# Three entries of a slot calendar moved: parts of y sooner, the last pair's values later, weight splits ahead of squares

## The chip, the cores and the metric

The kernel runs on one core of one Trainium2 chip. The metric is the device time of one execution in microseconds (us): before the change the median of 3 runs is 815.99 us (815.72 to 816.66).

## The reference

One decoder layer on x of 512 tokens and 2048 channels, in float32. What matters of it:

```python
h = rms_norm(x, norm_g)
a_val, a_glu, a_gate, q, k, v, b_gate = jnp.split(h @ w_in, SPLIT_POINTS, axis=-1)
u = a_val * jax.nn.sigmoid(a_glu)
u = causal_depthwise_conv(u, conv_w, conv_b)                   # 31 taps
u = jax.nn.silu(layer_norm(u, conv_norm_g, conv_norm_b))
y_a = (u @ conv_pw_w + conv_pw_b) * jax.nn.silu(a_gate)
o = dilated_attention_mixture(rms_norm(q), rms_norm(k), v)     # 16 heads of 64
y_b = o * jax.nn.silu(b_gate)
return x + jnp.concatenate([y_a, y_b], axis=-1) @ w_out
```

`w_in` is 2048 x 7168, `conv_pw_w` 1024 x 1024, `w_out` 2048 x 2048.

## The kernel before

**Products.** A float32 product is done as three float16 matmuls: both operands are scaled by a power of two and split into a high half (on ACT, an ACTIVATE copy to float16) and a low half (on DVE, what the copy left over), and `tri` (L414 to L416) adds high x high, high x low and low x high in PSUM. `split_hi` and `split_lo` (L298, L306) make `wh` and `wl` of a pass's weights. A pass is four blocks of 128 rows of a weight matrix by 512 columns. Its scale needs the sum of its squares (`measure`, L192, ACTIVATE into `junk`), and so do the scales of y.

**Order.** The program is written out by hand: nothing reorders it, and each engine takes its instructions in the order in which they are issued. The clock of that order is the slot, eight of them to a pass: a slot issues what is due in a calendar, what its pass has listed for it and some steps of the convolution branch, then six matmuls of 128x512 on PE. `after(n, fn)` puts `fn` into the calendar n slots on (at least one). In the loop over the plain passes (L1351) each slot takes two lists: `due`, from the calendar, and `extra`, the splits of the next pass's weights (high half at slot 0, low half at slot 2) and loads of the residual `res`. L1419 says which of the two comes first.

**Where the change sits.** The passes around it, in their order, are 52 to 55 (`bg` 1: the second half of the attention gate), 56 to 59 (`pw`: the pointwise projection of the convolution branch, 56 and 57 its first 512 columns, 58 and 59 its second), 60 and 61 (`wb` 2 and 3: rows 8 to 11 of y times `w_out`, plain, three matmuls to a block), and then four groups `wa` in Strassen's manner, seven products of halves instead of eight, whose weight blocks `ws`, `wsc` and `wsd` are sums made by DMAs that add (issued on GpSimd) and by DVE. The slots of `pw` start at 448, those of `wb` at 480, those of `wa` at 496.

**Names.** `cv` is the convolution's result in eight row blocks: the layer norm multiplies it by `lnrow` (DVE), applies SiLU (ACT, L609), and splits it into `u` (ACT L316, then DVE), which `pw` reads. Rows 8 to 11 of y are `y_b` of the first eight heads, in four tiles of `gate` ("b0"). `b0_parts` (L691) makes their halves: `plain` (L678) for `wb`, a high half on ACT (L688) and a low half on DVE for each of four tiles; and for `wa` the differences `ysum` of halves of these tiles (`y_sums`, L643, four pairs of subtractions on DVE), split by `block` (L663; ACT L675, then DVE) into four more parts. It asks for nothing but these tiles and the scale `yb0`, which is found by slot 360.

**Attention.** Heads go in pairs, a pair every 32 slots; pair 7, the last, begins at slot 450. Its scores (L741) come in two batches, at slots 450 and 453; DVE adds the table to them and takes them out of PSUM (`sx<-ps_s`). Then follow the exponentials (ACT L754), the two halves of the probabilities (`hl`: ACT L765, then DVE), and a transposing DMA for each head on SyncE (`turn`, L774) into `pt`. `values` (L782) are 60 thin matmuls of `pt` with v into `ps_o`; `put` multiplies the outcome by the gate on DVE (`gate<-ps_o`) and hands it to `put_y` (L623), which has ACT square it. When all twelve tiles of `y_a` and of the later `y_b` are squared, the scale `yabs` is found and `y_parts` (L701) makes the halves for `wa`. `end_pair` issues `values` and `put`; it is due when the next pair begins, and for pair 7 after `PERIOD - 2` slots, at 480.

**Buffers.** PSUM has four banks for `ps_l` (L102) and four for `ps_s` and `ps_o` (L103), which are taken in turn: a batch of scores waits until DVE has read what stood in its banks. Tiles of y, u, gate and cv rotate through one pool of 35 slots; halves of weights through 4 buffers, so that `wh` of the next pass waits until PE is done with the pass before this one.

Of the kernel before, what the change touches and what calls it, by code (L numbers as in the profile page):

```python
# [35 lines left out]
PERIOD = {0: 32, 1: 32}  # L36
# [50 lines left out]
def layer(ctx: ExitStack, tc: tile.TileContext, xt, w1, w2, w3, g_in, conv_w, conv_b,  # L87
# [31 lines left out]
    calendar = {}  # L119
    clock = [-1]  # L120

    def after(n, fn):

        calendar.setdefault(clock[0] + max(n, 1), []).append(fn)
# [126 lines left out]
    of_group = {}  # L251
# [46 lines left out]
    def split_hi(i):  # L298
        if i < n_plain:
            parts[i] = [part_pool.tile([P, KU, S], F16, name=n, tag="part") for n in ("wh", "wl")]  # L300
            A.activation(parts[i][0], raw[i], AF.Copy, scale=wscale[units[i][3:]][0])  # L301
# [4 lines left out]
    def split_lo(i):  # L306
        if i < n_plain:
            wh, wl = parts[i]
            V.scalar_tensor_tensor(wl, raw.pop(i), wscale[units[i][3:]][0], wh, op0=OP.mult, op1=OP.subtract)
            load(i + RING)  # L310
            after(11 if of_next(i) in SEVEN else 9, lambda: measure(i + RING))
# [110 lines left out]
    def evac_scale(group):  # L422

        if group not in escale:
            other = {"pw": "u", "wa": "yab", "wb": "yb0"}.get(group[0])
            e = escale[group] = small.tile([P, 1], F32, name="esc")
            G.tensor_tensor(e, wscale[group][1], scales[other][1] if other else xinv, op=OP.mult)
        return escale[group]
# [377 lines left out]
    def end_pair(pair):  # L806

        for fn in to_come.pop(pair, ()):
            fn()

    def attention(hf):
        start = max(clock[0] + 28, max(at_pair.values(), default=0) + PERIOD[0])
        start += (PHASE - start) % 8
        for p4 in range(4):
            at_pair[4 * hf + p4] = start + p4 * PERIOD[hf]

            def begin(pair=4 * hf + p4):
                end_pair(pair - 1)
                plan, values, put = two_heads(pair)
                to_come[pair] = values, put  # L820
                for n, fn in plan:
                    if n == 0:
                        fn()
                    else:
                        after(n, fn)
                after(PERIOD[hf] - 2 * (pair == 7), lambda: end_pair(pair))
            after(at_pair[4 * hf + p4] - clock[0], begin)


# [31 lines left out]
    def fetch_res(j):  # L861

        res[j] = wide_tile("res", [P, 2, S], F32)
        nc.sync.dma_start(res[j], rows_of(xt, j))
# [4 lines left out]
    def run_conv():  # L869

        pace = PACE_2 if 0 < min(at_pair.values(), default=0) <= clock[0] else PACE
        V.load = min(max(V.load - pace, -pace), 4 * pace)
        wait[0] -= 1
        while (V.load < 0 or wait[1]) and wait[0] <= 0:
            n = next(convolution, 1)
            if n:
                wait[0] = n
# [442 lines left out]
    def startup(n):  # L1320

        s, second = divmod(n, 2)
        todo = []
        if not second:
            if s + 3 < KU * n_exact:
                todo += [lambda: exact_hi(s + 3), lambda: exact_lo(s + 3)]
            if s + 2 < KC:
                todo.append(lambda: split_x(s + 2))
        if n == 0:
            for k in range(1, KC):  # L1330
                after(4 + (k - 1) * 26 // 14, lambda k=k: square_x(k))
            for n in range(KC):
                after(NORM_FROM + n * (70 - NORM_FROM) // KC, lambda k=n // 2 + 4 * (n // 8) + 4 * (n % 2): norm_x(k))
            for j in range(8):
                after(SUM_FROM + SUM_STEP * j // 2, lambda j=j: sum_x(j))
            g = token_rsqrt(xacc, D, RMS_EPS, rstd, rrow)
            for m in (32, 33, 36):
                after(m, lambda: next(g, None))
            for m, fn in ((21, x_consts), (40, score_consts), (37, u_consts)):
                after(m, fn)  # L1340
            after(8 * n_exact - 4, lambda: split_hi(n_exact))
            after(8 * n_exact - 3, lambda: split_lo(n_exact))
        return todo
# [3 lines left out]
    def due_now():  # L1347
        return [fn for n in sorted(n for n in calendar if n <= clock[0]) for fn in calendar.pop(n)]

    calendar.setdefault(8 * of_group["pw", 0][0] + 6, []).append(b0_parts)  # L1350
    for i in range(n_plain):  # L1351
        kind, g = group = units[i][3:]
        if group in SEVEN:
            if i == of_group[group][0]:
                plan = ahead.pop(i) + later
                later = []
                n_next = i + 4
                if units[n_next][3:] in SEVEN:
                    ahead[n_next] = input_products(n_next)
                    plan += [(n + 28, fn) for n, fn in ahead[n_next] if n < 0]  # L1360
                else:
                    plan = [(24, lambda: split_hi(n_next)), (25, lambda: split_lo(n_next))] + plan
                for n in range(28):
                    clock[0] = 8 * i + n + n // 7
                    for fn in due_now():
                        fn()
                    first = [fn for k, fn in plan if k == n]
                    for fn in first[:]:
                        if fn.__name__ != "matmuls":
                            fn()  # L1370
                    run_conv()
                    for fn in first:
                        if fn.__name__ == "matmuls":
                            fn()
                later = [(n - 28, fn) for n, fn in plan if n >= 28]
                if units[n_next][3:] not in SEVEN:
                    for n, fn in later:
                        after(8 * n_next + n - clock[0], fn)
                    later = []
                if kind == "k":  # L1380
                    attention(g)
            continue
        exact = i < n_exact
        if exact:
            order = [(None, None)] * 8
        else:
            order = [(m, hf) for m in range(4) for hf in range(2)]
            extra = [[] for _ in range(8)]
            if i == n_plain - 1:
                for n, fn in seven_parts(0):  # L1390
                    if n < 0:
                        extra[n].append(fn)
            if i + 1 < len(units) and units[i + 1][3:] in SEVEN:
                ahead[i + 1] = input_products(i + 1)
                for n, fn in ahead[i + 1]:
                    if n < 0:
                        extra[n].append(fn)
            else:
                extra[0].append(lambda: split_hi(i + 1))
                extra[2].append(lambda: split_lo(i + 1))  # L1400
            if i + 1 < len(units) and units[i + 1][3] == "wb":
                for m in range(2):
                    extra[4 * m].append(lambda m=m: fetch_res(2 * units[i + 1][4] + m))
            if kind == "pw" and i == n_plain - 3:
                for n in (2, 3):
                    extra[n].append(lambda n=n: evac_scale(("wb", n)))
            if (kind, g) == ("wb", 3):
                for m in range(2):
                    extra[4 * m].append(lambda m=m: fetch_res(m))
        if kind == "pw":  # L1410
            need = KU * units[i][2] + KU - 1
            while need not in u16:
                next(convolution)
        for n, (m, hf) in enumerate(order):
            clock[0] = 8 * i + n
            if exact:
                extra = {n: startup(clock[0])}
            due = due_now()
            for fn in extra[n] + due if exact else due + extra[n]:  # L1419
                fn()  # L1420
            run_conv()
            done = exact_matmuls(clock[0]) if exact else slot_matmuls(i, m, hf)
            if done:
                done()
        if kind == "k" and i == of_group[group][-1]:
            attention(g)
# [62 lines left out]
```

## Time and profile before

| | before |
|---|---|
| median of 3 runs | 815.99 us (815.72 to 816.66) |
| the profiled execution | 816.64 us |
| its span, first to last instruction | 814.5 us |
| mean granted TensorE clock | 0.998 |
| PE busy | 806.0 us |
| DVE busy | 706.8 us |
| ACT busy | 561.5 us |
| GpSimd busy | 136.8 us |

Times in the profile are us from the span's start; a line such as L414 is that of the code above. A row of the timeline is: start, duration, engine, line, operation, out<-in, shape and count; in brackets the idle time of the engine before it and who ended it. Rows of ACT and DVE overlap a little, and a matmul of 128x512 is shown with 0.38 us though they start 0.22 apart. A row of the windows is: stretch, its length, then the busy time of PE, its weight loads, DVE, ACT and GpSimd, the granted clock, the DMAs' share and GB/s. SPq rows are transfers that SyncE issues.

### The profile page before, as it was taken

The page shows a single profiled execution, that of the slowest core. Times are in us where ns is not written, and L with a number is a line of the kernel's source. Part 1 is how long each engine was busy: PE and PEld are TensorE (multiplying, and loading weights), DVE is VectorE, ACT ScalarE, POOL GpSimd, SP SyncE. Part 2 cuts the span into 40 slices and gives each one's busy share as a digit, 9 for nine tenths or more (in the row PEclk, how much of TensorE's full clock was granted, in tenths as well). Part 3 has the DMA queues.
Part 4 walks back from the last instruction along what each step waited for, and adds up shares of the span by engine and source line. Part 5 has one row for each costly group of instructions (what it writes and reads, how often), then busy time and mean ns, then how long its engine had stood idle before and what let it go on. Part 6 is the DMA issues. An engine that isn't in the chain of part 4 may idle for free.

```text
span 814.5 us, 13602 instructions
## 1 busy us (share of the span) xinstructions
PE 806.0 (99%) x5341; PEld 509.4 (63%) x5341; DVE 706.8 (87%) x1188; ACT 561.5 (69%) x788; POOL 136.8 (17%) x147
## 2 busy tenths in 40 slices
PE   9999999999999999999999999999999989999998
PEld 6887745888646854444444444444444446888887
DVE  6768999878989889999999989996579889978885
ACT  6667687577756688586747657497799849864641
POOL 0001021322224300004012010000200003423420
PEclk9999999999999999999999999999999999999999
DMA  9852346993874863526494624425361467898752
GB/s 338 330 233 98 109 104 137 144 248 55 315 149 100 148 261 113 123 93 164 142 181 130 151 97 137 135 89 133 104 168 63 126 213 195 162 259 201 130 102 68
DMA packets 100000, 127.19 MB, mean 156 GB/s; under 512 B 62560, under 2 KB 85344, under 8 KB 90720
## 3 DMA queue, kind: packets, MB, share of 16 engines
q1 hardware_dynamic: 80544, 107.37, 42.2%
q0 software_dynamic: 19104, 18.88, 16.2%
q8 instruction: 41, 0.67, 0.3%
q14 instruction: 23, 0.19, 0.1%
q10 hardware_dynamic: 288, 0.07, 0.0%
HBM read 88.56 MB, written 4.19 MB: 114 GB/s over the span
## 4 chain that ended last, share of the span: by engine, by line
PE 90%; DVE 3%; ACT 3%; DMA 2%; issue 1%; POOL 0%; SPq 0%; ACTq 0%; DVEq 0%
PE ps_l L414 24%; PE ps_l L415 23%; PE ps_l L416 23%; PE ps_l L895 10%; PE ps_s L416 2%; PE ps_s L415 2%; PE ps_s L414 2%; PE ps_o L782 2%; PE ps_s L741 2%; ACT junk L192 1%; DVE ws L82 1%; DMA wf<-w_dram 1%; DMA pt<-hl 1%; ACT sx L754 1%; DVE wl L82 1%
## 5 line engine op out<-in xcount | busy, mean ns | idle before, releaser
L82 DVE SCALAR_TENSOR_TENSOR cv<-u,cw,cv 128x511 f32<-128x511 f32 (+14 forms) x240 | 161.9, 727 | 0.4 <-ACT cv L552 0.4
L192 ACT ACTIVATE junk<-wf 128x2048 uint8<-128x2048 f32 x68 | 129.2, 1899 | 10.4 <-DMA wf<-w_dram 10.0
L414 PE MATMUL ps_l<-x,wh 128*128 128x512 f16 x320 | 121.3, 379 | 0.4 <-DVE glu L82 0.4
L416 PE MATMUL ps_l<-x,wl 128*128 128x512 f16 x320 | 121.3, 379 | 0.0
L415 PE MATMUL ps_l<-x,wh 128*128 128x512 f16 x320 | 121.3, 379 | 0.0
L301 ACT ACTIVATE wh<-wf,ws 128x2048 f16<-128x2048 f32 x42 | 83.8, 1994 | 53.3 <-PE ps_l L415 51.5
L82 DVE SCALAR_TENSOR_TENSOR wl<-wf,ws,wh 128x2048 f16<-128x2048 f32 x43 | 100.9, 2346 | 11.5 <-ACT wh L301 11.5
L414 PE MATMUL ps_l<-wh,x 128*128 128x512 f16 x256 | 97.1, 379 | 0.0
L416 PE MATMUL ps_l<-wh,x 128*128 128x512 f16 x256 | 97.0, 379 | 0.0
L415 PE MATMUL ps_l<-wl,x 128*128 128x512 f16 x256 | 97.0, 379 | 0.0
L82 DVE SCALAR_TENSOR_TENSOR ws<-wf,ws 128x1024 f16<-128x1024 f32 x70 | 89.1, 1278 | 7.3 <-ACT ws L1173 4.5
L414 PEld LDWEIGHTS <-wh 128*128 128x128 f16 x448 | 43.9, 98 | 51.5 <-issue 4.0
L416 PEld LDWEIGHTS <-wl 128*128 128x128 f16 x448 | 43.8, 98 | 51.1 <-DVE wl L82 1.9
L415 PEld LDWEIGHTS <-wh 128*128 128x128 f16 x448 | 43.8, 98 | 47.1 <-issue 0.8
L895 PE MATMUL ps_l<-xr,wr 128*128 128x512 f32 x288 | 69.4, 396 | 0.5 <-ACT xr L339 0.5
L895 PEld LDWEIGHTS ps_l<-xr,wr 128*128 128x128 f32 x288 | 53.9, 188 | 14.2 <-ACT xr L339 1.8
L206 POOL TENSOR_SCALAR ws<-ws 128x1 f32<-128x1 f32 x20 | 9.8, 488 | 309.1 <-DVE ws L82 308.7
L414 PEld LDWEIGHTS <-x 128*128 128x128 f16 x352 | 34.4, 98 | 32.5 <-issue 1.9
L416 PEld LDWEIGHTS <-x 128*128 128x128 f16 x352 | 34.4, 98 | 31.3
L415 PEld LDWEIGHTS <-x 128*128 128x128 f16 x352 | 34.4, 98 | 30.1
L1173 ACT ACTIVATE ws<-wf,ws 128x1024 f16<-128x1024 f32 x42 | 47.1, 1138 | 5.7 <-PE ps_l L416 4.8
L170 POOL TENSOR_TENSOR ss<-ss,half 128x8 f32<-128x8 f32 x16 | 31.5, 1970 | 116.8 <-DVE ss L82 116.6
(265 smaller groups left out, 1872.9 us busy)
## 6 DMA issues: line engine op xcount, KB each, us to landing
wf<-w_dram SPq DMA_DIRECT2D x72, 1024.0 KB, 5.2
wf<-wf POOLq DMA_DIRECT2D x30, 512.0 KB, 6.2
x<-xt_dram SPq DMA_DIRECT2D x16, 256.0 KB, 6.9
res<-xt_dram SPq DMA_DIRECT2D x8, 512.0 KB, 6.7
out_dram<-res SPq DMA_DIRECT2D x15, 256.0 KB, 3.7
wf<-w_dram SPq DMA_DIRECT2D x7, 512.0 KB, 7.2
wf<-wf POOLq DMA_DIRECT2D x12, 256.0 KB, 5.8
wf<-w_dram SPq DMA_DIRECT2D x2, 256.0 KB, 3.5
```

The costliest lines, as they stand in the source:

```text
L82: return getattr(self.engine, name)(out, src, *args, **kw)
L170: G.tensor_tensor(ap, ap, half.to_broadcast(list(ap.shape)), op=OP.pow)
L192: A.activation(junk[:, :n], src, AF.Square, scale=scale, accum_out=acc)
L206: G.tensor_scalar(scale, scale, 1e-30, 2.0 ** (-2 * top), op0=OP.max, op1=OP.mult)
L301: A.activation(parts[i][0], raw[i], AF.Copy, scale=wscale[units[i][3:]][0])
L414: T.matmul(ps, ah, bh, start=first, stop=False, skip_group_check=more)
L415: T.matmul(ps, ah, bl, start=False, stop=False, skip_group_check=more)
L416: T.matmul(ps, al, bh, start=False, stop=last, skip_group_check=more)
L741: T.matmul(ps[i, a], qk["q", hf][p4 // 2][rows, p4 % 2, q, i * P:w], qk["k", hf][p4 // 2][rows, p4 % 2, k, :w], start=n == 0, stop=n == 2)
L782: T.matmul(po[rows, i * P:(i + 1) * P], vs[hf][j // 2][:, j % 2, 2 * p4 + a, vp * DH:(vp + 1) * DH], got["t", a][:, pp * (ALL // P) + FROM ...
L895: T.matmul(banks[group, m], wt[:, a, m * P:(m + 1) * P], xk[b], start=k == 0 and a == b == 0, stop=k == KC - 1 and a == 1)
L1173: A.activation(t[:, 0], block(name, pair), AF.Copy, scale=wscale[group][0])
```

## The change

Three edits:

```diff
-                after(PERIOD[hf] - 2 * (pair == 7), lambda: end_pair(pair))
+                after(PERIOD[hf] - (pair == 7), lambda: end_pair(pair))
...
-    calendar.setdefault(8 * of_group["pw", 0][0] + 6, []).append(b0_parts)
+    calendar.setdefault(8 * of_group["pw", 0][0] - 10, []).append(b0_parts)
...
-            for fn in extra[n] + due if exact else due + extra[n]:
+            for fn in extra[n] + due if exact or kind == "wb" else due + extra[n]:
```

`b0_parts` starts at slot 438 instead of 454, in the last pass of the gate, where the layer norm's last steps run. Pair 7's values are issued at slot 481 instead of 480, so behind the first slot of `wb`. In the two `wb` passes the splits of the next weights stand ahead of what the calendar has for the slot. Nothing is added or left out; GpSimd's and SyncE's instructions stand as before.

On DVE, at the layer norm's end and pair 7's first scores. The number in a name tells one buffer from another (u_6090 before and u_6114 after are the same part of u); `gate<-ps_o` takes out the values of pair 6, `ISA sx` the scores. Before:

```order
L82 SCALAR_TENSOR_TENSOR u_6050<-cv,us,u_6050 128x512
L82 SCALAR_TENSOR_TENSOR gate<-opair,osc,gate 128x512
L82 TENSOR_TENSOR cv<-cv,lnrow 128x512
L82 SCALAR_TENSOR_TENSOR u_6071<-cv,us,u_6071 128x512
L82 TENSOR_TENSOR cv<-cv,lnrow 128x512
L82 SCALAR_TENSOR_TENSOR u_6090<-cv,us,u_6090 128x512
L82 SCALAR_TENSOR_TENSOR gate<-ps_o,osc,gate 128x512
L82 ISA sx,st_6183<-ps_s,tab 128x512
```

And now, from the second `gate` of the piece above on:

```order
L82 TENSOR_TENSOR cv<-cv,lnrow 128x512
L82 SCALAR_TENSOR_TENSOR y_6069<-gate,yb0s,y_6069 128x512
L82 TENSOR_TENSOR ysum<-gate,ysum 128x256 x2
L82 SCALAR_TENSOR_TENSOR u_6089<-cv,us,u_6089 128x512
L82 TENSOR_TENSOR cv<-cv,lnrow 128x512
L82 TENSOR_TENSOR ysum<-gate 128x256 x2
L82 SCALAR_TENSOR_TENSOR y_6108<-ysum,yb0s,y_6108 128x2x256
L82 TENSOR_TENSOR ysum<-gate,ysum 128x256 x2
L82 SCALAR_TENSOR_TENSOR u_6114<-cv,us,u_6114 128x512
L82 SCALAR_TENSOR_TENSOR y_6124<-ysum,yb0s,y_6124 128x2x256
L82 SCALAR_TENSOR_TENSOR gate<-ps_o,osc,gate 128x512
L82 ISA sx,st_6213<-ps_s,tab 128x512
```

Three low halves of y and three pairs of subtractions came in here; three more low halves and one more pair stand above the piece. The last two low halves stand between the two batches of `sx`.

On PE, at the end of pass 59 (`u_6213` and `u_6248` are the last part of u) and the first slot of pass 60. Before:

```order
L415 MATMUL ps_l<-u_6213,wh 128x512
L416 LDWEIGHTS wl
L416 MATMUL ps_l<-u_6213,wl 128x512
L782 LDWEIGHTS v_4692
L782 MATMUL ps_o<-pt,v_4692 64x128
```

And now:

```order
L415 MATMUL ps_l<-y_6011,wh 128x512
L416 LDWEIGHTS wl
L416 MATMUL ps_l<-y_6011,wl 128x512
L782 LDWEIGHTS v_4692
L782 MATMUL ps_o<-pt,v_4692 64x128
```

The values of pair 7 stand behind the six matmuls of the first slot of pass 60, three on `y_5999` and three on `y_6011`.

On ACT, in the `wb` passes (`junk,ysum` are squares of y, `junk,wsum` of weights, `wh` the high half of pass 61's weights, L995 that of the first plain weights of `wa`). Before:

```order
L192 ACTIVATE junk,ysum<-gate 128x512
L192 ACTIVATE junk,wsum<-wf 128x2048
L192 ACTIVATE junk,ysum<-gate 128x512 x4
L301 ACTIVATE wh<-wf,ws 128x2048
L192 ACTIVATE junk,wsum<-wf 128x2048
L675 ACTIVATE y_6742<-ag_5125,yabs 128x256
```

And now:

```order
L192 ACTIVATE junk,ysum<-gate 128x512
L192 ACTIVATE junk,wsum<-wf 128x2048
L192 ACTIVATE junk,ysum<-gate 128x512 x2
L301 ACTIVATE wh<-wf,ws 128x2048
L192 ACTIVATE junk,ysum<-gate 128x512 x2
L192 ACTIVATE junk,wsum<-wf 128x2048
L995 ACTIVATE wh<-wf,ws 128x2048
L675 ACTIVATE y_6755<-ag_5125,yabs 128x256
```

Two squares of y now stand behind pass 61's `wh`, and the plain weights of `wa` ahead of the first part of y.

## The prediction

> **What bounds the kernel now.** I read the page's busy times first, then the windows, then PE's waits, then the timeline around each wait.
>
> ```profile
> PE 806.0 (99%) x5341; PEld 509.4 (63%) x5341; DVE 706.8 (87%) x1188; ACT 561.5 (69%) x788; POOL 136.8 (17%) x147
> ```
>
> ```profile
> 640.00:660.00 20.00, 16.74 (x115) 8.66 (x115) 18.77 (x33) 13.42 (x20) 1.59 (x5) 0.93 0.74 200
> 660.00:800.00 140.00, 140.00 (x1201) 116.22 (x1197) 122.72 (x175) 91.05 (x117) 45.02 (x44) 1.00 0.76 171
> ...
> 644.00:648.00 4.00, 3.14 (x15) 1.47 (x16) 3.97 (x9) 4.00 (x7) 0.00 (x0) 1.00 0.55 162
> ...
> 655.00:658.00 3.00, 0.72 (x13) 0.58 (x13) 2.97 (x7) 0.72 (x2) 0.00 (x0) 0.86 1.16 263
> 658.00:661.00 3.00, 3.00 (x54) 2.74 (x51) 2.32 (x6) 0.73 (x2) 0.00 (x0) 0.58 0.98 395
> ```
>
> PE is the bound: no idle time in 140 us of the windows' second row, 3.26 us idle in the first. There the granted clock, the third number from the end, also falls: 0.86, then 0.58, which makes (0.14 + 0.42) x 3 x 2 = 3.4 us at half clock. The two waits behind that, in PE's timeline, with the same product one attention pair earlier for comparison:
>
> ```profile
> 611.01 1.87 PE L782 MATMUL ps_o<-pt,v 128*64 128x128 f16 x60
> ...
> 644.86 0.39 PE L416 MATMUL ps_l<-u,wl 128*128 128x512 f16 x1 [0.98 <-DVE wl L82]
> 645.08 0.38 PE L414 MATMUL ps_l<-u,wh 128*128 128x512 f16 x1
> ...
> 657.41 3.31 PE L782 MATMUL ps_o<-pt,v 128*64 128x128 f16 x59 [2.28 <-DMA pt<-hl]
> ```
>
> PE waits 0.98 us for the low half of pass 59's weights, and 2.28 us for pair 7's turned probabilities. After the second wait the 59 products take 3.31 us, where pair 6's 60 took 1.87: the half clock costs 1.44 us more. What can be had here is 0.98 + 2.28 + 1.44 = 4.70 us.
>
> **What the moved parts of y cost.** They are eight high halves on ACT, eight low halves on DVE and four pairs of subtractions on DVE. The work is the same, but it now stands among the layer norm's last steps. One row alone and one of two in a row give what each further one adds:
>
> ```profile
> 619.94 1.32 ACT L688 ACTIVATE y<-gate,yb0s 128x512 f16<-128x512 f32 x2
> ...
> 631.67 0.71 ACT L688 ACTIVATE y<-gate,yb0s 128x512 f16<-128x512 f32 x1
> ```
>
> ```profile
> 624.19 1.41 DVE L82 SCALAR_TENSOR_TENSOR y<-gate,yb0s,y 128x512 f16<-128x512 f32 x2
> ...
> 629.23 0.74 DVE L82 SCALAR_TENSOR_TENSOR y<-gate,yb0s,y 128x512 f16<-128x512 f32 x1
> ...
> 630.61 0.74 DVE L82 TENSOR_TENSOR ysum<-gate 128x256 f32<-128x256 f32 x2
> ...
> 633.08 0.88 DVE L82 TENSOR_TENSOR ysum<-gate,ysum 128x256 f32<-128x256 f32 x2
> ```
>
> A high half adds 1.32 - 0.71 = 0.61 us, a low half 1.41 - 0.74 = 0.67. A pair of subtractions adds 0.74 or 0.88 less the 0.07 by which DVE's rows overlap (2 x 0.74 - 1.41): 0.67 and 0.81.
>
> By the order, six low halves and all four pairs now stand on DVE ahead of pair 6's `gate<-ps_o`, and that is in-order: 6 x 0.67 + 2 x 0.67 + 2 x 0.81 = 7.0 us. DVE's idle time on the way there can take some of it up:
>
> ```profile
> 607.61 0.75 DVE L82 SCALAR_TENSOR_TENSOR u<-cv,us,u 128x512 f16<-128x512 f32 x1 [1.14 <-ACT u L316]
> ...
> 611.13 0.75 DVE L82 SCALAR_TENSOR_TENSOR u<-cv,us,u 128x512 f16<-128x512 f32 x1 [1.50 <-ACT u L316]
> ...
> 613.02 0.75 DVE L82 SCALAR_TENSOR_TENSOR u<-cv,us,u 128x512 f16<-128x512 f32 x1 [0.54 <-ACT u L316]
> 613.69 0.75 DVE L82 SCALAR_TENSOR_TENSOR gate<-ps_o,osc,gate 128x512 f32<-128x512 f32 x1
> 614.35 0.68 DVE L82 CUSTOM_DVE_ANT_0 sx<-ps_s,tab 128x512 f32<-128x512 f32 x1
> ...
> 614.96 0.69 DVE L82 CUSTOM_DVE_ANT_0 sx<-ps_s,tab 128x512 f32<-128x512 f32 x1
> ```
>
> ```profile
> 617.55 1.16 PE L741 MATMUL ps_s<-qk,qk 64*128 64x128 f16 x18
> ```
>
> Idle are 1.14 + 1.50 + 0.54 = 3.2 us, so `gate` comes 3.8 us later (7.0 if none is taken up). Who waits for that: pair 7's second batch of scores, four of the four banks of `s_ps`. One of these is still held by `ps_o` until `gate` has read it, two by the first batch until the two `sx` rows have. They end at 614.44, 615.03 and 615.65; 3.8 us later that is 618.2, 618.8 and 619.45. PE wants the first at 617.55 and the last some 0.7 us into the 1.16, so it waits 0.7 us and then, at 617.55 + 0.7 + 0.7 = 618.95, another 0.5: **a new wait of 1.2 us** that the trace of before does not have. Its ends: nothing, if DVE is less than 2.6 us later, and 3.9 + 0.5 = 4.4 us, if none of the idle time is taken up. I take 1.2, since DVE's three idle stretches all wait for ACT's `u`, behind which there is now other DVE work to do first.
>
> ACT gets 8 x 0.61 = 4.9 us in the same stretch; two of the eight (619.94) stood ahead of pass 58's `wh` already, so 3.7 us are new there:
>
> ```profile
> 603.64 0.63 ACT L192 ACTIVATE junk<-gate 128x512 uint8<-128x512 f32 x1 [0.91 <-DVE gate L82]
> ...
> 609.06 0.63 ACT L192 ACTIVATE junk<-gate 128x512 uint8<-128x512 f32 x1 [0.91 <-DVE gate L82]
> ...
> 622.52 2.00 ACT L301 ACTIVATE wh<-wf,ws 128x2048 f16<-128x2048 f32 x1 [1.26 <-PE ps_l L415]
> ...
> 640.43 1.99 ACT L301 ACTIVATE wh<-wf,ws 128x2048 f16<-128x2048 f32 x1
> ```
>
> Idle are 0.91 + 0.91 + 1.26 = 3.1 us, so ACT is 0.6 us late at 622.52, or up to 2.4 if the two waits for `gate` stay. That `wh` waits for PE anyway, which is 1.2 us late itself: 1.2 it is.
>
> Pass 57 needs the last `u` next. From 617.48 to 621.20 DVE had one `wl` and four subtractions; two low halves more (1.34) now stand there, too:
>
> ```profile
> 617.48 2.34 DVE L82 SCALAR_TENSOR_TENSOR wl<-wf,ws,wh 128x2048 f16<-128x2048 f32 x1
> ...
> 621.20 0.74 DVE L82 SCALAR_TENSOR_TENSOR u<-cv,us,u 128x512 f16<-128x512 f32 x1
> ```
>
> ```profile
> 624.70 0.38 PE L415 MATMUL ps_l<-u,wh 128*128 128x512 f16 x1
> ```
>
> After the later `sx` (619.45) and a `u` (0.67), `wl` starts at 620.1, the last `u` at 620.1 + 3.72 + 1.34 = 625.2 and ends at 625.9. PE wants it at 624.70 + 1.2 = 625.9: 0.1 us at most. **New waits: 1.3 us.**
>
> **What goes.** Between 622.52 and 640.43 ACT works without a pause worth naming, and four of the moved high halves were there: 4 x 0.61 = 2.4 us less. Pass 59's `wh` starts at 640.43 + 1.2 - 2.4 = 639.2, 1.2 us sooner, and its `wl` with it, while PE gets there 1.3 us later. The wait of 0.98 had 0.98 to make good and gets 2.5: it goes (at worst half of it stays, if DVE's own backlog holds `wl`).
>
> ```profile
> 646.02 4.66 SPq L774 DMA_TRANSPOSE pt<-hl  x1
> 650.74 0.58 SPq L864 DMA_DIRECT2D res<-xt_dram  x1
> 651.41 3.87 SPq L774 DMA_TRANSPOSE pt<-hl  x1
> ```
>
> Pair 7's two turns follow each other on SP without a gap; the second, issued at 651.41, is what the values at 657.41 waited for, 6.0 us later. The first follows the last low halves, which stand right behind pass 59's `wl`; both turns come up to 1.2 us sooner, and land at 656.2 to 657.4. PE asked at 657.41 - 2.28 = 655.13. Now it asks 0.98 sooner and 1.3 later, and one slot on, which is six matmuls of 0.22 (from 644.86 to 645.08): 655.13 - 0.98 + 1.3 + 1.3 = 656.75. It waits 0 to 0.65 us; I take 0.1. A wait of 0.98 us had no fall of the clock behind it (644 to 648: granted 1.00), so I count the 1.44 as gone.
>
> [...]
>
> **What must come along.** From 660 on PE has no wait, but little to spare:
>
> ```profile
> 738.13 0.74 DVE L82 SCALAR_TENSOR_TENSOR wsd<-wf,wjs,wsd 128x512 f16<-128x512 f32 x1
> ```
>
> ```profile
> 739.32 0.27 PE L416 MATMUL ps_l<-y,wsd 128*128 128x256 f16 x1
> ```
>
> ```profile
> 658.78 0.63 ACT L192 ACTIVATE junk<-gate 128x512 uint8<-128x512 f32 x1 [2.06 <-DVE gate L82]
> ...
> 663.63 1.99 ACT L301 ACTIVATE wh<-wf,ws 128x2048 f16<-128x2048 f32 x1
> ```
>
> This `wsd` is done at 738.87 and used at 739.32: 0.45 us. What PE gains ahead of it is lost there unless DVE is as much sooner. DVE's work there is a queue that starts with pass 61's `wl`, whose `wh` stood behind all the last squares until 663.63. Now it stands behind the second square of the four: free at 658.78 + 0.7 = 659.5 by the old times, 4.1 us sooner, more than PE's gain. I count the third edit at nothing by itself, and as what keeps the gain; the squares, one slot later, have the sum of y to feed, which PE now asks one slot later too.
>
> **Sum.** -4.70 + 1.3 + 0.1 = -3.3 us. The profiled execution took 816.64 (span 814.5), 0.65 above the median of 815.99; against the median that is **812.7 us**.
>
> **The rivals.**
> *No new wait.* If DVE is less than 2.6 us late at `gate`, all of the 4.70 is had: 811.3. For it: 3.2 us idle in DVE and 3.1 in ACT; against it: 7.0 us of work. Chance 0.14.
> *The clock falls anyway.* [...] Against it: pair 6's 60 products at 1.87 us. Chance 0.07.
> *The next bound is DVE at 739.* If its queue does not start sooner, PE gets 0.45 us and waits for the rest: 815.5. Against it: the 4.1 us at pass 61's `wh`. Chance 0.12.
> *Slower.* ACT and DVE wait for each other's halves, none of the idle time is taken up, and PE waits 4.4 us at pair 7's scores. That is longer than the wait that halved the clock; 3.4 us at half clock cost 1.7 more, and a second such stretch, if the wait reaches into it, 0.4 of it: 4.4 + 2.1 - 4.70 = +1.8, 817.8. It decides from new waits and lost clock of 4.70, so from a DVE some 5.6 us late. Chance 0.07.
>
> **How the numbers follow.** My forecast has 0.60. Its own range is 811.9 (the new wait at half) to 813.7 (0.65 at the values, 0.5 at `wl`). With the two rivals of 811.3 and 814.1 this makes 811.2 to 814.3, with 0.81 in it. A measurement of this kernel tells about 0.2%, 1.6 us, from no change. Faster by more: 0.60 + 0.14 + 0.07 = 0.81; within it 0.12; slower by more 0.07.
>
> **What would show it.** Right: no wait for `pt` over 0.7 us, none for pass 59's `wl`, the clock at 1.00 from 655 to 661, a wait of about 1.2 us at L741 near 618 put down to DVE, `gate<-ps_o` near 617.5, and no idle time of PE behind 660. Wrong: no wait at 618 (first rival), a PE wait for `wsd` near 736 (third), a clock under 1 near 618 (fourth).

## The result, and the profile after

The changed kernel takes 812.76 us (median of 6, 812.37 to 814.07) beside 816.24 for the kernel before (median of 6, 814.37 to 816.8; the three runs shown above are among them). The ratio is 0.9963, with a 95% interval of 0.9951 to 0.9976: 3.0 us faster by the ratio, 3.5 by the medians, 2.0 to 4.0 by the interval. The profiled execution took 812.95, its span 811.2 us.

The page of the changed kernel, its line of busy times:

```profile
PE 805.5 (99%) x5341; PEld 508.8 (63%) x5341; DVE 707.2 (87%) x1188; ACT 561.3 (69%) x788; POOL 136.2 (17%) x147
```

The work is the same; the span is 3.3 us shorter because PE waits less and no longer runs at half clock (granted 1.00 from 655 to 661, where it was 0.86 and 0.58). All waits of PE in the changed kernel from 600 us on (operation, what it waited for and from whom: us in total, times, longest):

```profile
PE ps_s L741 <- DVE st L82: 0.3, 1, 0.3
PE ps_o L782 <- DMA pt<-hl: 0.2, 1, 0.2
PE ps_s L741 <- DVE gate L82: 0.2, 1, 0.2
```

The row for `wl` (L416) is gone, that for `pt` is down from 2.28 to 0.2, and two rows at the scores (L741) are new. The windows of the changed kernel, columns as above:

```profile
640.00:660.00 20.00, 19.79 (x143) 9.71 (x142) 18.06 (x31) 13.70 (x18) 0.00 (x0) 1.00 0.77 210
655.00:658.00 3.00, 2.79 (x53) 1.75 (x53) 2.97 (x7) 1.12 (x3) 0.00 (x0) 1.00 1.11 275
658.00:661.00 3.00, 3.00 (x34) 1.61 (x29) 2.96 (x7) 2.80 (x5) 0.00 (x0) 1.00 0.99 392
660.00:800.00 140.00, 140.00 (x1206) 117.52 (x1205) 120.85 (x171) 88.86 (x116) 44.58 (x44) 1.00 0.76 170
```

From 640 to 660 PE is idle for 0.21 us where it was 3.26, and the granted clock is 1.00 where it was 0.86 and 0.58. Behind 660 PE still has no idle time. The two places in PE's timeline, after:

```profile
617.64 0.23 PE L741 MATMUL ps_s<-qk,qk 64*128 64x128 f16 x1
618.07 0.89 PE L741 MATMUL ps_s<-qk,qk 64*128 64x128 f16 x12 [0.20 <-DVE gate L82]
619.28 0.48 PE L741 MATMUL ps_s<-qk,qk 64*128 64x256 f16 x5 [0.33 <-DVE st L82]
619.70 0.39 PE L414 MATMUL ps_l<-u,wh 128*128 128x512 f16 x1
...
656.75 1.83 PE L782 MATMUL ps_o<-pt,v 128*64 128x128 f16 x59 [0.21 <-DMA pt<-hl]
```

The product that follows the scores began at 618.64 before, 1.09 us behind their first matmul:

```profile
618.64 0.39 PE L414 MATMUL ps_l<-u,wh 128*128 128x512 f16 x1
```

Now it begins 619.70 - 617.64 = 2.06 behind it. So the new wait costs PE 0.97 us, of which the brackets show 0.53. The 59 values take 1.83 us where they took 3.31. What stands behind both places, on DVE after the change:

```profile
617.27 0.74 DVE L82 SCALAR_TENSOR_TENSOR gate<-ps_o,osc,gate 128x512 f32<-128x512 f32 x1
617.93 0.68 DVE L82 CUSTOM_DVE_ANT_0 sx<-ps_s,tab 128x512 f32<-128x512 f32 x1
...
625.17 0.74 DVE L82 SCALAR_TENSOR_TENSOR u<-cv,us,u 128x512 f16<-128x512 f32 x1
...
641.73 2.35 DVE L82 SCALAR_TENSOR_TENSOR wl<-wf,ws,wh 128x2048 f16<-128x2048 f32 x1 [3.14 <-ACT wh L301]
```

On ACT after the change, pass 58's `wh`, the first exponential of pair 7, and the `wh` of passes 59 and 61:

```profile
623.66 1.99 ACT L301 ACTIVATE wh<-wf,ws 128x2048 f16<-128x2048 f32 x1
...
628.16 0.49 ACT L754 ACTIVATE sx<-sx,st,sc 128x128 f32<-128x128 f32 x1 [1.21 <-DVE st L82]
...
639.72 1.99 ACT L301 ACTIVATE wh<-wf,ws 128x2048 f16<-128x2048 f32 x1
...
657.51 1.99 ACT L301 ACTIVATE wh<-wf,ws 128x2048 f16<-128x2048 f32 x1
```

And the two turns of pair 7 on SyncE's queue:

```profile
645.30 4.77 SPq L774 DMA_TRANSPOSE pt<-hl  x1
...
650.80 3.94 SPq L774 DMA_TRANSPOSE pt<-hl  x1
```

The reader sees here the chain that the prediction followed: pair 6's `gate` is 3.6 us later (617.27 for 613.69), the scores wait for it, ACT then waits 1.21 us for the late scores, pass 59's `wh` is still 0.7 sooner (639.72 for 640.43), and so are the turns (0.7 and 0.6).

### The profile page after: what moved, and what is told of

It reads as the page before. It is cut to its first block, busy times and chain, and to the rows that moved or that the text cites. A ratio compares the mean times of both kernels' runs of the same rounds, so it can differ in the third digit from the quotient of the medians.

```text
span 811.2 us, 13603 instructions
## 1 busy us (share of the span) xinstructions
PE 805.5 (99%) x5341; PEld 508.8 (63%) x5341; DVE 707.2 (87%) x1188; ACT 561.3 (69%) x788; POOL 136.2 (17%) x147
## 4 chain that ended last, share of the span: by engine, by line
PE 92%; DVE 4%; ACT 2%; DMA 1%; issue 1%; POOL 0%; ACTq 0%; DVEq 0%
PE ps_l L414 24%; PE ps_l L415 24%; PE ps_l L416 24%; PE ps_l L895 10%; PE ps_s L415 2%; PE ps_s L414 2%; PE ps_s L416 2%; PE ps_o L782 2%; PE ps_s L741 2%; DVE ws L82 1%; DMA pt<-hl 1%; DVE wl L82 1%; ACT junk L192 0%; DMA wf<-w_dram 0%; DVE cv L82 0%
## 5 line engine op out<-in xcount | busy, mean ns | idle before, releaser
L416 PE MATMUL ps_l<-x,wl 128*128 128x512 f16 x320 | 121.3, 379 | 0.0
L416 PE MATMUL ps_l<-wh,x 128*128 128x512 f16 x256 | 97.0, 379 | 0.0
L416 PEld LDWEIGHTS <-wl 128*128 128x128 f16 x448 | 43.8, 98 | 50.0 <-DVE wl L82 0.4
L416 PEld LDWEIGHTS <-x 128*128 128x128 f16 x352 | 34.4, 98 | 31.3
```

The costliest lines, as they stand in the source:

```text
L416: T.matmul(ps, al, bh, start=False, stop=last, skip_group_check=more)
```

## The experiments

The three edits are numbered as in the diff: 1, the values one slot on; 2, `b0_parts` 16 slots sooner; 3, the splits first. The theory was that of the prediction: edits 1 and 2 take away PE's waits and with them the half clock, edit 2 pays about 1 us at the scores, edit 3 by itself does nothing but keeps the gain. `wsd` below is always the one of the prediction, whose product has little time to spare; the spare time is the start of that product less the end of `wsd`, 0.45 us before. The rivals were that the half clock does not hang on that wait, that DVE's queue behind 660 caps the gain, and that the moved parts cost more than they bring. Medians in us; the ratio is to the kernel before on the same chip.

| run | median | before | ratio (95%) |
|---|---|---|---|
| values_later_alone (edit 1) | 814.38 | 816.15 | 0.998 (0.9971 to 0.9988) |
| parts_sooner_alone (edit 2) | 813.90 | 816.15 | 0.9968 (0.9956 to 0.9981) |
| splits_first_alone (edit 3) | 816.21 | 816.15 | 1.0003 (0.9995 to 1.0012) |
| without_splits_first (1 and 2) | 812.94 | 816.15 | 0.9956 (0.9942 to 0.9969) |
| without_parts_sooner (1 and 3) | 813.42 | 816.39 | 0.9968 (0.9955 to 0.998) |
| without_values_later (2 and 3) | 814.03 | 816.39 | 0.9976 (0.9966 to 0.9985) |
| sums_at_old_place | 811.83 | 816.39 | 0.9948 (0.9934 to 0.9961) |
| parts_ten_slots_sooner | 818.59 | 816.39 | 1.0032 (1.0019 to 1.0045) |
| sums_old_place_no_splits_first | 812.96 | 816.13 | 0.9964 (0.9951 to 0.9977) |
| sums_old_place_values_two_on | 811.80 | 816.13 | 0.9949 (0.9935 to 0.9962) |

**Edit 1 alone** (the changed kernel with the other two undone):

```diff
-    calendar.setdefault(8 * of_group["pw", 0][0] - 10, []).append(b0_parts)
+    calendar.setdefault(8 * of_group["pw", 0][0] + 6, []).append(b0_parts)
...
-            for fn in extra[n] + due if exact or kind == "wb" else due + extra[n]:
+            for fn in extra[n] + due if exact else due + extra[n]:
```

> Pair 7's values at slot 481, the other two edits left out. Theory: the wait for pt falls from 2.28 to 2.28 - 1.30 = 0.98 us, too short for the half clock, so 1.30 + 1.44 = 2.7 us are had at the values; the 0.98 us for pass 59's wl stays. Behind it DVE's queue, which still starts behind all the squares, is only about 2 us sooner, with 0.45 us to spare at wsd, so PE waits up to 0.5 us near 737: 2.2 to 2.7 us faster than before. Rival 1 (no cap by DVE): 2.7 us, no wait for wsd. Rival 2 (the half clock does not hang on this wait): 1.3 us, with a granted clock under 0.9 near 658.

Measured: 1.8 us faster by the medians, 2.1 by the spans of the traces (814.5 and 812.4), less than expected. PE's waits in this run:

```profile
PE ps_o L782 <- DMA pt<-hl: 1.0, 1, 1.0
...
PE ps_l L416 <- DVE wl L82: 1.0, 1, 1.0
...
PE ps_s L204 <- ACT junk L192: 0.3, 1, 0.3
```

The wait for `pt` falls from 2.28 to 1.0, and the clock stays at 1.00 from 655 to 661, so a wait of 1.0 us is short enough here: the turned probabilities need not be there in time. A part of the gain goes into a wait for the sum of the squares of y (L204). Its reason is on ACT:

```profile
661.50 0.63 ACT L192 ACTIVATE junk<-gate 128x512 uint8<-128x512 f32 x1 [2.06 <-DVE gate L82]
662.13 1.99 ACT L301 ACTIVATE wh<-wf,ws 128x2048 f16<-128x2048 f32 x1
664.03 0.61 ACT L192 ACTIVATE junk<-gate 128x512 uint8<-128x512 f32 x1
```

Edit 1 alone already puts the last square, that of the values' own tile, behind pass 61's `wh`: before, that `wh` was the one that stood behind all of them. At `wsd` nothing is left to spare: it is done at 737.12, and its product starts at 737.18, 0.19 us behind the matmul before it, where those around it follow at 0.11. So DVE holds PE up there by 0.08 us, at the lower end of the 0 to 0.5 that the theory had.

**Edit 2 alone** (edits 1 and 3 undone):

```diff
-                after(PERIOD[hf] - (pair == 7), lambda: end_pair(pair))
+                after(PERIOD[hf] - 2 * (pair == 7), lambda: end_pair(pair))
```

> b0_parts 16 slots sooner, the other two edits left out. Theory: the 0.98 us for pass 59's wl go, about 1.0 us of new waits at pair 7's scores come, PE is where it was at pass 60; pair 7's turns are some 0.6 us sooner, so the wait for pt is 1.4 to 1.8 us instead of 2.28. If that still halves the clock: 0.5 to 0.9 us faster than before; if not: PE gains another 1.4, of which DVE at wsd lets some 0.5 to 1 through: 1 to 2 us faster. Rival (the moved parts pay by themselves, as the change's main gain): over 2.5 us faster.

Measured: 2.25 us faster, between the theory's 2 and the rival's 2.5. The theory had DVE hold some of the gain back at `wsd`; the spare time there is 736.67 - 735.50 = 1.17 us, so it held nothing back. The values and the clock there:

```profile
656.24 1.83 PE L782 MATMUL ps_o<-pt,v 128*64 128x128 f16 x59 [1.57 <-DMA pt<-hl]
...
655.00:658.00 3.00, 1.76 (x59) 1.67 (x58) 2.56 (x6) 0.72 (x2) 0.00 (x0) 1.00 1.08 296
```

A wait of 1.57 us has no half clock behind it either. The scores wait 0.3 and 0.2, as in the whole change, and the wait for pass 59's `wl` is gone: both belong to edit 2.

**Edit 3 alone** (edits 1 and 2 undone):

> Weight splits ahead of the calendar's work in the two wb passes, the other two edits left out. Theory: within 0.3 us of before, since no PE wait hangs on it; DVE is 2 us or more sooner at wsd, so what PE has to spare there grows from 0.45 to over 2 us. Rival (the edit gains by itself): over 0.5 us faster.

Measured: no difference in time, as expected. The values still wait, and the clock still falls:

```profile
657.08 2.85 PE L782 MATMUL ps_o<-pt,v 128*64 128x128 f16 x59 [2.30 <-DMA pt<-hl]
...
655.00:658.00 3.00, 0.92 (x28) 0.92 (x29) 2.96 (x7) 0.73 (x2) 0.00 (x0) 0.95 1.12 256
658.00:661.00 3.00, 3.00 (x40) 2.12 (x36) 2.77 (x6) 2.56 (x4) 0.00 (x0) 0.50 0.98 395
661.00:664.00 3.00, 3.00 (x15) 1.36 (x14) 1.77 (x5) 2.43 (x6) 0.00 (x0) 0.99 0.48 184
```

The other half of the expectation, a `wsd` 2 us sooner or more, failed. Pass 61's `wh`, a row of DVE on the way, `wsd` and its product:

```profile
659.07 1.99 ACT L301 ACTIVATE wh<-wf,ws 128x2048 f16<-128x2048 f32 x1
...
690.42 1.23 DVE L82 TENSOR_TENSOR wf<-wf 128x1024 f32<-128x1024 f32 x1 [1.14 <-DMA wf<-wf]
...
738.04 0.75 DVE L82 SCALAR_TENSOR_TENSOR wsd<-wf,wjs,wsd 128x512 f16<-128x512 f32 x1
...
739.11 0.27 PE L416 MATMUL ps_l<-y,wsd 128*128 128x256 f16 x1
```

The DVE row before the change:

```profile
690.36 1.22 DVE L82 TENSOR_TENSOR wf<-wf 128x1024 f32<-128x1024 f32 x1 [0.79 <-DMA wf<-wf]
```

That `wh` is 4.6 us sooner (659.07 for 663.63), `wsd` 0.09 (738.04 for 738.13), and the spare time is 739.11 - 738.79 = 0.32. DVE does not run through from pass 61's `wl` to `wsd`. That `wl` is 1.7 us sooner (663.97 for 665.65), and near 690, where DVE waits for a sum of weights that a DMA makes, it goes on at the time of before. The longest of its later waits, near 734, is for a scale from GpSimd (3.32 us in before, 3.41 here); `wsd` starts 3.32 us behind the end of that wait in both.

**The whole change without edit 3**, to see whether DVE's queue caps the gain:

```diff
-            for fn in extra[n] + due if exact or kind == "wb" else due + extra[n]:
+            for fn in extra[n] + due if exact else due + extra[n]:
```

> The first two edits, the third left out. Theory: PE's waits up to pass 61 are those of the whole change; pass 61's wh stands behind the last squares, 3.5 us later than in the whole change, its wl some 2 us later, and PE meets DVE at wsd: a wait of 0.2 to 1.5 us near 736, so 0.2 to 1.5 us slower than the whole change. Rival (the third edit does nothing): the time of the whole change, no wait for wsd.

Measured: 812.94, the time of the whole change, with a span of 810.4 and no wait for `wsd`. Its `wsd` and the first product that reads the low half, beside the same two of the whole change:

```profile
733.67 0.74 DVE L82 SCALAR_TENSOR_TENSOR wsd<-wf,wjs,wsd 128x512 f16<-128x512 f32 x1
...
735.16 0.27 PE L416 MATMUL ps_l<-y,wsd 128*128 128x256 f16 x1
```

```profile
734.21 0.74 DVE L82 SCALAR_TENSOR_TENSOR wsd<-wf,wjs,wsd 128x512 f16<-128x512 f32 x1
...
735.89 0.27 PE L416 MATMUL ps_l<-y,wsd 128*128 128x256 f16 x1
```

The spare time is 735.16 - 734.41 = 0.75 us without edit 3 and 735.89 - 734.95 = 0.94 with it, where it was 0.45 before. Neither is a bound. ACT without edit 3, at pass 61's `wh`:

```profile
658.90 0.63 ACT L192 ACTIVATE junk<-gate 128x512 uint8<-128x512 f32 x1 [2.06 <-DVE gate L82]
659.53 1.99 ACT L301 ACTIVATE wh<-wf,ws 128x2048 f16<-128x2048 f32 x1
661.42 0.61 ACT L192 ACTIVATE junk<-gate 128x512 uint8<-128x512 f32 x1
```

And before the change, the last square ahead of it, that of `pw`'s last tile:

```profile
663.00 0.63 ACT L192 ACTIVATE junk<-gate 128x512 uint8<-128x512 f32 x1 [0.67 <-DVE gate L82]
```

That square is the one at 658.90 here, and `wh` begins at 659.53 and not at 663.63. Of these 4.1 us 0.7 are no gain: this execution was that much ahead of before's already at pair 7's scores, which began at 616.87 for 617.55. Edit 1 brings 1.4 of the rest (662.13 in the run of edit 1 alone, its scores at 617.49): the square of the values' tile no longer stands in front, and DVE's row for the last square no longer stands behind the one that waits for the values (0.68 us at 660.76 before). Edit 2 brings 2.0: DVE works without a pause from pass 59's `wl` to that row, this `wl` is 0.8 us sooner against the scores, and two of the moved low halves (1.39 us at 646.17 before) no longer stand between. Edit 3 makes `wh` 2.8 us sooner again by the same count (657.51 in the whole change, whose scores began at 617.64), which nothing here needs.

**The whole change without edit 2, and without edit 1** (each undone as in the diffs above):

> Values at slot 481 and weight splits first, b0_parts at its old place. Theory: as the values later alone, but with DVE sooner at wsd: the 0.98 us for pass 59's wl and about 0.98 us for pt stay, nothing halves the clock, no wait at the scores near 618 and none for wsd: 2.7 us faster than before, 0.5 to 0.9 us slower than the whole change. Rival (the moved parts are the main gain): under 1.5 us faster than before.

> b0_parts 16 slots sooner and weight splits first, pair 7's values at slot 480. Theory: the new waits at the scores (about 1.0 us) eat the 0.98 us of pass 59's wl, and the wait for pt is 1.4 to 1.8 us. If the clock halves behind it: 0.5 to 0.9 us faster than before; if not: 1.9 to 2.3 us, since nothing caps it at wsd. Rival: the time of the whole change, if the turns alone come soon enough.

Measured: 3.0 and 2.4 us faster, near what was expected (2.7, and 1.9 to 2.3). Without edit 2 PE waits 0.97 for pass 59's `wl` and 1.08 for `pt`, without edit 1 it waits 1.54 for `pt` and 0.5 at the scores; the clock is 1.00 in both. The edits do not add up (1.8 and 2.25 alone, 3.2 together), mainly because each of the two alone already takes the 1.44 us of half clock away, which can be had once.

**Only the plain parts sooner**: the halves of `gate` for `wb` 16 slots sooner, the sums of y and their parts where they were, edits 1 and 3 as in the change:

```diff
-            after(6 + 3 * k, lambda k=k: y_sums("d", y, k, k + 2))
+            after(16 + 6 + 3 * k, lambda k=k: y_sums("d", y, k, k + 2))
...
-                after(9 + 3 * k + n, lambda name=name, k=k: block(name, k, s))
+                after(16 + 9 + 3 * k + n, lambda name=name, k=k: block(name, k, s))
```

> The whole change, but of b0_parts only the four plain parts are 16 slots sooner; the four pairs of subtractions and the four parts made of them stand where they stood before. Theory (the new wait at pair 7's scores comes from the 7.0 us that DVE has to do ahead of gate<-ps_o): only 4 x 0.67 = 2.7 us are left there, less than the 3.2 us of idle time, so gate is on time within 0.5 us, both waits near 618 go and 0.9 to 1.1 us are had: 1.0 us faster than the whole change, 811.7 or so. pass 59's wl must still be on time: four high halves are back on ACT ahead of its wh, 2.4 us, against some 1 us of room and the 1.0 us that PE now comes sooner, so up to 1 us of that can be lost again. Rival (the wait is due to the four plain parts or to ACT): the time of the whole change.

Measured: 811.83, the lowest median together with that of the last run below (811.80); the traced execution, with a span of 809.4, was its fastest, and 0.73 us ahead of the whole change's already at pair 7's scores (616.91 for 617.64). Pair 6's `gate` and the scores behind it, then the values:

```profile
614.29 0.75 DVE L82 SCALAR_TENSOR_TENSOR gate<-ps_o,osc,gate 128x512 f32<-128x512 f32 x1
```

```profile
616.91 1.16 PE L741 MATMUL ps_s<-qk,qk 64*128 64x128 f16 x18
...
654.99 1.83 PE L782 MATMUL ps_o<-pt,v 128*64 128x128 f16 x59 [0.36 <-DMA pt<-hl]
```

The 18 matmuls stand in one row again: no wait at the scores. `gate` is 1.2 us later against the scores than before (614.29 and 616.91 for 613.69 and 617.55), more than the 0.5 expected, and nothing waits for it. So the new wait is the price of the sums alone, and what the change needs of edit 2 is the plain parts, which leave ACT and DVE before pass 59's `wh`. The intervals of this run and of the whole change overlap by a little (0.9934 to 0.9961, 0.9951 to 0.9976); the missing 0.97 us at the scores is in the trace, and 812.76 - 811.83 = 0.93 fits it.

**Ten slots sooner instead of 16** (the whole change, the calendar's entry moved):

```diff
-    calendar.setdefault(8 * of_group["pw", 0][0] - 10, []).append(b0_parts)
+    calendar.setdefault(8 * of_group["pw", 0][0] - 4, []).append(b0_parts)
```

> The whole change, but b0_parts 10 slots sooner (slot 444) instead of 16. Theory: the same work, in the same stretch of the program, now stands between pair 7's first and second scores and ahead of the splits of pass 58: the parts' high halves on ACT wait for subtractions that stand on DVE behind pair 6's gate, and pass 58's wh and the squares of the weights stand behind them. PE waits 2 us or more for pass 58's wl near 635 and for the weights' squares near 638: 3 to 6 us slower than the whole change, about the time of before. Rival (only the amount of work counts): within 1 us of the whole change.

Measured: 2.2 us slower than before and 5.8 slower than the whole change, with PE's two waits at the places that were expected. PE and ACT in this run:

```profile
636.15 0.39 PE L416 MATMUL ps_l<-u,wl 128*128 128x512 f16 x1 [2.32 <-DVE wl L82]
639.12 0.16 PE L204 MATMUL ps_s<-wsum,ones 128*128 128x4 bf16 x1 [1.93 <-ACT junk L192]
```

```profile
629.22 0.72 ACT L675 ACTIVATE y<-ysum,yb0s 128x512 f16<-128x512 f32 x1 [4.32 <-DVE ysum L82]
629.84 1.99 ACT L301 ACTIVATE wh<-wf,ws 128x2048 f16<-128x2048 f32 x1
```

Here a high half of a sum stands on ACT in front of pass 58's `wh`, and waits 4.32 us for DVE's subtraction, which stands behind the second `sx` batch. The `wh` behind it is 6.2 us later than in the whole change (629.84 for 623.66), its `wl` as well, PE waits twice, and the granted clock falls to 0.68 from 640 to 644. As in the prediction's slower rival, ACT and DVE wait for each other's halves; but that rival had PE wait at the scores, and here these stand in one row (617.28, `gate` at 615.84) and the waits are at pass 58.

**The fastest version without edit 3, and with the values another slot on:**

```diff
-            for fn in extra[n] + due if exact or kind == "wb" else due + extra[n]:
+            for fn in extra[n] + due if exact else due + extra[n]:
```

> The kernel with the sums at their old place (plain parts 16 slots sooner, sums of y and their parts where they were, values one slot on), now without the third edit. By the theory that the third edit is worth nothing once the values stand one slot on (the values' square then stands behind pass 61's wh by itself, and wh comes 2.0 us later without a wait of PE, 659.53 against 657.51): within 1.2 us of the kernel with all of it, 811 to 812.6, and no wait of PE for wsd. By the rival that the third edit keeps the gain once PE is still further ahead: PE waits 0.7 us or more for wsd near 732, and it takes 813 or more.

```diff
-                after(PERIOD[hf] - (pair == 7), lambda: end_pair(pair))
+                after(PERIOD[hf], lambda: end_pair(pair))
```

> The kernel with the sums at their old place, and pair 7's values one more slot on (two later than before the change). By the theory, the 0.4 us for the turned probabilities goes, since six matmuls of 0.22 more stand ahead of the values, but the last square of y comes 1.3 us later and PE waits 0.3 to 0.5 us for the sum of y (L204) instead: 811.3 to 812.3, the same as without this step. By the rival that the wait for the turned probabilities is the last one that PE has there: 0.4 us or more faster, and no wait at L204.

Measured without edit 3: 812.96, between the two numbers that were expected, and no wait for `wsd` in the list. But the spare there is nearly used up, `wsd` against the first low product:

```profile
734.30 0.75 DVE L82 SCALAR_TENSOR_TENSOR wsd<-wf,wjs,wsd 128x512 f16<-128x512 f32 x1
```

```profile
735.27 0.27 PE L416 MATMUL ps_l<-y,wsd 128*128 128x256 f16 x1
```

735.27 - 735.05 = 0.22, where the version with edit 3 has 734.13 - 732.58 = 1.55. So here edit 3 does put DVE further ahead of PE; what it is worth there this run leaves open, since the two ran beside different runs of before and their intervals overlap.

Measured with the values two slots on: 811.80, the same as without that step. The wait for `pt` is gone, and in its place stands the one for the squares:

```profile
PE ps_s L204 <- ACT junk L192: 0.8, 1, 0.8
```

The theory's reason holds (the last square comes later with the values), its size was 0.3 to 0.5.

## Why the prediction was right, and where it was not

**The wait for pass 59's `wl` (0.98).** Right, and edit 2's doing: it goes in the two runs with edit 2 but without edit 1, and stays in the two with edit 1 but without edit 2. Its `wh` came at 639.72, not 639.2. The step took ACT to work without a pause until then; it had one, 1.21 us for the late scores, against which 0.54 us of a pause at 639.80 that before had are gone.

**The wait for `pt` (2.28, 0.1 left).** Right: 0.21 is left, and the values begin at 656.75, the time at which the prediction had PE ask for them. Two errors cancel in this: the turns came 0.6 to 0.7 us sooner, not up to 1.2, and PE lost less ahead of them.

**The half clock (1.44).** Right that it goes, and in these runs it goes with the wait for `pt`, not with PE's thin products: the clock is 1.00 in all runs with a wait of up to 1.57 us there, with the same 59 products behind it (1.83 us in the changed kernel), and falls in the profiles of before and of edit 3 alone, with 2.28 and 2.30. Of the 57 timed executions of the kernels with edit 1, edit 2 or both (the one of ten slots left out) none has a mean granted clock under 0.999; of the 55 of before and of edit 3 alone 44 have. The rival that the clock falls anyway fell; its 814.1 is the forecast with the 1.44 added. No trace shows that 1.44 behind a shorter wait: behind one of 0.21 us the 59 values take 1.83.

**The new wait at the scores (1.2).** Right in mechanism, a little too big: 0.97. `gate` came at 617.27, predicted 617.5. The ends of that bound were 0 and 4.4; the choice, DVE's idle time taken up, held.

**The last `u` (0.1).** No wait. The row stands at 625.17, predicted 625.2.

**The sum.** -3.3 predicted; the spans differ by 814.5 - 811.2 = 3.3, the profiled executions by 816.64 - 812.95 = 3.7, the medians by 816.24 - 812.76 = 3.5. Term by term: -0.98 - 2.07 - 1.48 + 0.97 = -3.6. From the first matmul of the scores to the product of `wsd` PE took 739.32 - 617.55 = 121.77 us before and 735.89 - 617.64 = 118.25 after, 3.5 less, so the terms leave nothing out there.

**Edit 3 as what keeps the gain.** This step failed, in two places. The prediction gave the 4.1 us by which pass 61's `wh` would be sooner to edit 3 alone; undone, the time is the same, and that `wh` is 3.4 us sooner by the other two edits, which shorten the queue of DVE and ACT in front of it. And the prediction had DVE's queue to `wsd` start with pass 61's `wl`: in the run of edit 3 alone `wh` is 4.6 us sooner and `wsd` 0.09, since DVE waits on the way, for a DMA's sum near 690 and for GpSimd's scale near 734. In the whole change the wait near 690 ends at 686.07 for 690.36; what made that sum sooner was not followed, so why `wsd` kept up with PE stays open. The step cost nothing in the sum, which held edit 3 at nothing, but the rival of 815.5 had a chance (0.12) for a wrong reason. The meeting of PE and DVE that it feared shows only in edit 1 alone, with 0.08 us.

**The rivals.** "No new wait" (811.3) was wrong for this change, and is what sums_at_old_place does: 811.83, with 0.36 us left at `pt`. "Slower" (817.8) needs the halves to wait for each other; at 16 slots they do not (`gate` is 3.6 us late, not 5.6), at ten slots they do (818.59), though with the waits at pass 58 and none at the scores. No trace shows the 0.4 us that its sum has for a second stretch at half clock: the three in which the clock fell show one stretch of 3.4 us each.

## What to carry to other kernels

Moving work out of the way of a late transfer paid here only as far as the wait behind it: half of the moved work (the plain halves) brought the gain (811.83 us with them alone), and the other half (the sums, needed only by `wa`) only brought a wait at its new place (0.97 us at the scores). Where an engine takes its instructions in the order of issue, as in these traces, a moved step is read by what stands behind it, not by its own length: one subtraction in a bad place held a weight split for 4.32 us, and the kernel was slower than before (818.59 us for 816.39). Before a second engine's queue is called a cap, or an edit is said to lift it, follow the queue row by row: waits on the way took back all of the 4.6 us that edit 3 alone had gained at its head.

## What the runs showed of the hardware

The half clock is not there in every execution. Of 44 timed executions of the kernel before beside these runs, 33 had a mean granted clock of 0.997 or 0.998 and a median of 816.41 us, 11 had 1.00 and a median of 814.86: it is worth 1.55 us where it falls. It fell in 19 of 21 on one chip, 8 of 13 on another and 6 of 10 on a third; edit 3 alone, on the first, had it in 11 of 11. The executions without it were not traced; if their wait was as long as in the one that was, a wait of 2.28 us does not always bring the fall. So about 1.5 of the 3.5 us that the change brings are brought only in about three executions of four. The rest is the waits: 814.86 - 812.76 = 2.10, and 0.98 + 2.07 - 0.97 = 2.08. In the profile of before the granted clock is 0.50 in each half microsecond from 657.5 to 660.5, and 1.00 from 661 on. In the profile of edit 3 alone the fall lasted (0.05 + 0.50 + 0.01) x 3 x 2 = 3.4 us, as in the profile of before and in that of ten slots ((0.48 + 0.09) x 3 x 2 from 639 to 645, behind waits of 2.32 and 1.93). The length is the same in the three, the products in it are not: the 59 values took 2.85 us in edit 3 alone and 3.31 in before, and in edit 3 alone the rest of it fell on the wide products behind, the first three of which are shown with 0.61, 0.63 and 0.58 us instead of 0.38.

The traces show the clock fall behind a wait of 2.28 us (before) and of 2.30 (edit 3 alone), and not behind one of 1.57 (edit 2 alone). In the run of ten slots it is 1.00 from 636 to 639, behind the wait of 2.32 that ends at 636.15, and 0.68 from 640 to 644, behind the one of 1.93 that ends at 639.12. What decides between these was not measured: whether it is the length of the one wait or what stands around it, the runs do not tell.
